# One GLA output sum's split moved into four small-pool buffers, and the first MLP block's last products placed behind LN1's transposes of token tiles three and four

## The chip, the core and the metric

The kernel runs on one core of a Trainium2 chip. The metric is the device time of one execution in microseconds. It is 865.92 us before the change, the median of three runs (865.25 to 866.03). Lower is better.

## What is computed

The reference is one decoder layer on 512 tokens of width 1024, in float32. Cut to what matters here:

```python
h = layer_norm(x, ln_in_g, ln_in_b)
q_g, k_g, v_g, r_g, a_lr, q_lat, kv_lat, gate_logits = split(h @ w_in)
y_gla = (rms_norm(gla(q_g, k_g, v_g, log_a)) * silu(r_g)) @ w_o_gla
q  = rms_norm(q_lat) @ w_q_b            # 8 heads, 128 without and 64 with rope
kv = rms_norm(kv_lat) @ w_kv_b          # 8 heads, keys 128 and values 128
y_mla = softmax_attention(q, kv) @ w_o_mla
mix = (g_gla * y_gla + g_mla * y_mla) @ w_out
h1 = layer_norm(ALPHA * h + mix, ln1_g, ln1_b)
out = layer_norm(ALPHA * h1 + square(relu(h1 @ w_ff1)) @ w_ff2, ln2_g, ln2_b)
```

## The kernel before

**Arithmetic.** Every float32 matrix product is made of three TensorE products. An operand is split into a high part `hi` (a rounding copy on ScalarE, ACT in the profile) and a low part `lo` (a subtraction on VectorE, DVE). The products are hi by hi, hi by lo and lo by hi. They are the three lines L280 to L282 (features by tokens, `gemm_fm`), L318 to L320 (tokens by features, `gemm_tm`) and L1320 to L1322 (the units below).

**Weights as a stream.** All weights stand in one list, `stream`, in the order of use. `fetch` (L196) allocates a raw tile `wraw` and issues its load on SyncE's queue (SP in the profile). `pump` (L211) fetches two entries ahead and splits one or two entries ahead of the entry in use. The raw tiles rotate through three buffers, the split parts `whi` and `wlo` through two each. An entry's `home` names the buffers that receive its split. Home "w" is `whi` and `wlo`. Home "r" is `wraw` twice, so the two parts of such an entry sit in two of the three raw buffers until its last product has read them. Pool A has large tiles (4 KB per partition), pool B has 22 small ones (2 KB per partition).

**Units.** Some matrix products (`unit`, L1297) use seven products of half-size blocks in place of eight, with operands that are sums of blocks. `yg`, the GLA output projection with `w_o_gla`, is one of them. Its products are named "11", "t1", "22", "t2", "t3", "21" and "t4", each with two column groups g = 0 and 1. A name with t stands for a sum of weight blocks. Such a sum is made in a tile `wq` and then split like loaded weights. With `cut` = 2 the split of a `yg` entry is made in two halves.

**Order around the first edit.** The stream has `yg` "22" and "t2", then the rope part of the queries (`qr`, group 0), then `yg` "t3" (groups 0 and 1), then for the first pair of MLA heads `qn` (two entries), `kn` and `mv` (one each, from `w_kv_b`), then `yg` "21", which is loaded as it is, then `qr` group 1. In the trace, `latT` are the normalised latents, which SP loads back from memory (L1435) into tiles of pool A. `ogT` are the operands of `yg`. `QS<-q` (L1071) are 16 copies of the roped queries, issued on GpSimd's queue (POOL). `mv`'s products are L318 to L320, those of `kn` and `qn` L280 to L282.

**Order around the second edit.** After the mixer, the rows `res` are normalised by LN1 two token tiles at a time. `ln1(1)` (L1540) does token tiles three and four. DVE and POOL make the statistics, DVE normalises the rows, and `ln_transpose` (L509) transposes them on TensorE (L516, PE in the profile), eight channel blocks of two transposes each. ACT makes the high part `h`, DVE the low part. Meanwhile TensorE multiplies the first block of `w_ff1` with the first 256 tokens (L1556, 8 contraction blocks of 12 products of 256 columns) and then with the last 256 tokens, whose operands those transposes deliver.

```python
    t_ln = spawn(ln1(1))
    accs = gemm_fm(PL["f1", 0, 0], h1T, T, None, toks=slice(0, 256))
    finish(t_ln)
```

A `spawn`ed generator is advanced at every `tick`, so its instructions stand between those of the products. A scheduler then sets the order on each engine by its own estimates, with data dependences and the edges that `tc.issue_after` adds.

Of the kernel before, what the change touches and what calls it, by code (L numbers as in the profile page):

```python
# [11 lines left out]
F32R = mybir.dt.float32r  # L12
# [7 lines left out]
P = 128  # L20
T = 512
# [31 lines left out]
def tile_hybrid_block(ctx: ExitStack, tc: tile.TileContext, I, out, dbg=None):  # L53
# [12 lines left out]
    def nm(s):  # L66
        uid[0] += 1
        return f"{s}_{uid[0]}"
# [4 lines left out]
    def A(shape, dt=F32, n="a"):  # L73
        tag, bufs = ("C", 8) if n in TAG_C else (n, TAG_W[n]) if n in TAG_W else ("A", 24)
        return pa.tile(shape, dt, tag=tag, bufs=bufs, name=nm(n))

    def B(shape, dt=F32, n="b"):
        return pb.tile(shape, dt, tag="B", name=nm(n))
# [8 lines left out]
    def MM(n="mm"):  # L87
        return pm.tile([P, T], F32, tag="mm", name=nm(n))
# [4 lines left out]
    def f(ap):  # L93
        return ap.bitcast(F32)
# [28 lines left out]
    mm = nc.tensor.matmul  # L123
# [46 lines left out]
    st = {"dma": 0, "spl": 0, "gates": ()}  # L170
# [25 lines left out]
    def fetch(n):  # L196
        while st["dma"] < min(len(stream), n):
            e = stream[st["dma"]]
            st["dma"] += 1
            if "src" in e:  # L200
                continue
            raw = A([P, e["nk"], T * 2 // e["nk"]], F32, e.get("at", "wraw"))
            for sl, src, cw in e["dmas"]:
                if cw is None:
                    dst = raw[:, sl, :e["n"]]
                else:
                    dst = raw[:, sl[0], sl[1]].rearrange("p (h c) -> p h c", c=cw)
                nc.sync.dma_start(dst, src)
            e["raw"] = raw

    def pump(i):  # L211
        fetch(i + 1 + DMA_AHEAD)
        while st["spl"] < min(len(stream), i + 2 + SPLIT_AHEAD):
            e = stream[st["spl"]]
            if st["spl"] > i + e.get("ahead", SPLIT_AHEAD) and not e["res"]:
                break
            nk, n = e["nk"], e["n"]
            hi, lo = [A([P, nk, T * 2 // nk], F32R, w) for w in HOME["a" if e["res"] else e.get("home", "w")]]
            raw = e["src"]() if "src" in e else e.pop("raw")
            with ExitStack() as gates:  # L220
                for g in e.get("gates") or st["gates"] or (st.get("pt", ()) if e.get("late") else ()):
                    gates.enter_context(tc.issue_after(g.ins))
                step = 1 if e.get("fine") else nk // e.get("cut", 1)
                for k in [slice(i, i + step) for i in range(0, nk, step)]:
                    st["ins"] = act(hi[:, k, :n], raw[:, k, :n], AF.Copy)
                    st["lo"] = vtt(lo[:, k, :n], raw[:, k, :n], f(hi[:, k, :n]), op=ALU.subtract)
            st["gates"] = ()
            e["w"] = (hi, lo)
            if "post" in e:
                e["post"](raw)  # L230
            if "post2" in e:
                later[st["spl"] + 2] = lambda p=e["post2"], r=raw: p(r)
            later.pop(st["spl"], lambda: None)()
            st["spl"] += 1
# [32 lines left out]
    def part(x, i, c):  # L267
        return x[i][:, c] if isinstance(x, tuple) else x[:, i, c]

    def gemm_fm(pl, xs, n, evac, width=None, toks=slice(0, T), accs=None, guard=None):  # L270
        na = n // P
        accs = accs or [MM() for _ in range(na)]
        for k in range(pl["nk"]):
            hi, lo = weights(pl, k)
            xh, xl = part(xs[k], 0, toks), part(xs[k], 1, toks)
            first, last = k == 0, k == pl["nk"] - 1
            for a in range(na):
                c = slice(a * P, (a + 1) * P)
                o = accs[a][:, toks]
                mm(o, hi[:, c], xh, start=first, stop=False)  # L280
                mm(o, hi[:, c], xl, start=False, stop=False)  # L281
                mm(o, lo[:, c], xh, start=False, stop=last)  # L282
            if not last:
                tick(width)
        if guard:
            guard()
        if evac is not None:
            for a in range(na):
                evac(a, accs[a])
                if a == na // 2 - 1:  # L290
                    pump(pl["idx"][-1] + 1)
        tick(width)
        return accs
# [45 lines left out]
    PL = {}  # L339
# [16 lines left out]
    for op, _ in RW:  # L356
        for hf in range(2):
            PL["r"].append(len(stream))
            e = {"nk": 2, "n": T, "res": False, "ahead": 2, "home": "wwwwrwrwrwwwrw"[2 * RW.index((op, _)) + hf]}
# [11 lines left out]
    HOME = {"w": ("whi", "wlo"), "r": ("wraw", "wraw"), "a": ("xh", "xl")}  # L371
# [29 lines left out]
    def plan_unit(*seq):  # L401
        for key, op in seq:
            for g in range(UNITS[key][2]):
                PL[key, op, g] = len(stream)
                e = {"nk": 4, "n": 256, "res": False}
                if key in ("g1","yg"):
                    e["cut"] = 2
                if (key, op, g) == ("yg", "t3", 1):
                    e["home"] = "r"
                if op[0] != "t" and (op, key) not in HELD:  # L410
                    e["dmas"] = [(slice(0, 4), u_src(key, int(op[0]) - 1, int(op[1]) - 1, g), None)]
                else:
                    e["src"] = lambda q=(key, (op, g)): WQ[q]
                    if key == "g0" and op in ("t1", "t2"):
                        e["ahead"], e["home"] = 2, "wr"[g]
                if op == ("t1" if key == "g0" else "22"):
                    e["post"] = lambda raw, q=(key, "t1", "t2", g): u_sum(*q, WQ[q[0], ("22", q[3])] if q[0] == "g0" else raw)
                    if key == "f1":
                        e["post2"] = lambda raw, q=(key, "12", "t3", g): u_sum(*q, raw)
                elif op == "21" and key == "yg":  # L420
                    e["post"] = lambda raw, g=g: u_sum("yg", "t2", "t4", g, raw)
                elif op == "t2" and key == "g1":
                    e["post"] = lambda raw, g=g: u_acc("g1", "t2", "t4", g, "21")
                elif op == "t2" and key != "yg":
                    e["post2" if key == "f1" else "post"] = lambda raw, q=(key, "t2", "t4", g): u_sum(*q, WQ[q[0], ("21", q[3])])
                stream.append(e)
# [82 lines left out]
    def ln_transpose(rows, g, b, outs, hf, alt=False, n="h0"):  # L509
        tk = slice(hf * 256, (hf + 1) * 256)  # L510
        for k in range(NK):
            if len(outs) <= k:
                outs.append(A([P, 2, T], F32R, n) if n == "h0" else (B([P, T], F32R, n), B([P, T], F32R, n)))
            p = MM() if alt and k in (4, 5) else PX()
            for i in range(2):
                tp = nc.tensor.transpose(p[:, i * P:(i + 1) * P], rows[2 * hf + i][:, k * P:(k + 1) * P],  # L516
                                         identJ if hf and n == "h0" else ident)
            if n == "h0" and k == 1:
                st["tp"] = tp
            tmp = B([P, 256], F32, "lnt")  # L520
            hi, lo = part(outs[k], 0, tk), part(outs[k], 1, tk)
            ha = act(hi, p[:, :256], AF.Identity, scale=g[:, k:k + 1], bias=b[:, k:k + 1])
            if (alt or n == "h1") and k % 2:
                act(tmp, p[:, :256], AF.Identity, scale=g[:, k:k + 1], bias=b[:, k:k + 1])
            else:
                vts(tmp, p[:, :256], g[:, k:k + 1], b[:, k:k + 1], op0=ALU.mult, op1=ALU.add)
            hd = vtt(lo, tmp, f(hi), op=ALU.subtract)
            if n == "h1":
                st["ln"] = (ha, hd)
            elif hf and k == 5:  # L530
                st["h0"] = (ha, hd)
            yield hd
# [691 lines left out]
    for hf in range(2):  # L1224
# [8 lines left out]
        for i in range(2):  # L1233
            gemm_tm([PL["lat", i]], hT, half, ev_lat(i), tts=(2 * hf, 2 * hf + 1), guard=lat_guard if i and not hf else None,
                    held=i and not hf)
# [245 lines left out]
    class Lazy:  # L1481
        def __getitem__(self, h):
            while omT[h] is None:
                tick(2)
            return omT[h]
# [18 lines left out]
    res = []  # L1504
# [33 lines left out]
    h1T = []  # L1538
# [14 lines left out]
    finish(t_ln)  # L1553
    st["gates"] = st["ln"]
    t_ln = spawn(ln1(1))
    accs = gemm_fm(PL["f1", 0, 0], h1T, T, None, toks=slice(0, 256))  # L1556
    finish(t_ln)

    def residual1():
# [147 lines left out]
    for ci in range(FC):  # L1707
# [3 lines left out]
        if ci == 0:  # L1711
            lo = stream[PL["f1", 0, 0]["idx"][2]]["w"][1]
# [32 lines left out]
        else:  # L1745
# [31 lines left out]
            tt, r, bst = 3, res[3], S([P, 4, 6], F32, "bst4")  # L1777
# [3 lines left out]
            for c0, n in ((0, T), (T, 256), (T + 256, 256)):  # L1781
                last = c0 > T
                acc = end if last else MM()[:, :n]
                ws = slice(c0 % T, c0 % T + n)
                for k in range(nb):
                    hi, lo = weights(PL["f2last"][c0 // T], k)
                    xh, xl = hid[k][:, 0, tt * P:], hid[k][:, 1, tt * P:]
# [58 lines left out]
```

## Time and profile before

| what | value |
|---|---|
| median of 3 runs | 865.92 us (865.25 to 866.03) |
| the profiled execution's own time | 866.7 us |
| its span, first to last instruction | 864.9 us |
| PE busy | 852.7 us, 99% |
| DVE busy | 657.8 us, 76% |
| ACT busy | 494.5 us, 57% |
| POOL busy | 136.0 us, 16% |
| HBM traffic over the span | 142 GB/s |
| granted TensorE clock, mean | 0.998 |

A row of the timeline gives the start in us from the beginning of the span, the duration in us, the engine, the line, the operation, what it writes and reads, its form and a count. In brackets stands the idle time of the engine just before it and what ended that. SPq and POOLq are the queues that issue DMAs. Matmuls overlap each other, so the pace of TensorE is read from the starts and not from the durations.

### The profile page before, as it was taken

The numbers are of one execution on the slowest core, as the hardware profiler recorded it, in microseconds if no ns is written. First come the engines' busy times: TensorE is split into PE (matmuls) and PEld (weight loads), VectorE is DVE, ScalarE is ACT, GpSimd is POOL, SyncE is SP. The second block draws the span as 40 slices with busy tenths as digits, with TensorE's granted clock in tenths as the row PEclk, the third lists the DMA queues.
The fourth block names the chain that finished last, engine by engine and source line by source line (L and its number), as shares of the span: only waits on it lengthen the run. The fifth ranks groups of instructions, "written<-read, shape, count | busy, mean of one in ns | idle before, by whom it ended". The sixth has DMA issues, their size and how long they took to land.

```text
span 864.9 us, 13264 instructions
## 1 busy us (share of the span) xinstructions
PE 852.7 (99%) x4887; PEld 752.6 (87%) x4887; DVE 657.8 (76%) x1169; ACT 494.5 (57%) x891; POOL 136.0 (16%) x179
## 2 busy tenths in 40 slices
PE   8999999999999999999999999999999999999996
PEld 7988888889999998988888889988888888889985
DVE  7767889977578967997856978985567546897865
ACT  7456977655576854565745334475466446766820
POOL 1530001110222103030000021005301520141000
PEclk9999999999999999999999999999999999999999
DMA  9995946696649817133146455009912990499312
GB/s 319 228 213 159 341 153 163 213 264 214 147 145 242 204 32 187 50 104 98 37 176 214 126 166 184 1 0 272 253 59 51 299 218 17 102 244 234 112 62 75
DMA packets 101231, 137.94 MB, mean 159 GB/s; under 512 B 13201, under 2 KB 66116, under 8 KB 101168
## 3 DMA queue, kind: packets, MB, share of 16 engines
q1 hardware_dynamic: 76512, 91.35, 33.9%
q0 software_dynamic: 22784, 41.10, 22.8%
q10 hardware_dynamic: 1872, 4.66, 1.4%
q8 instruction: 38, 0.62, 0.3%
q14 instruction: 25, 0.20, 0.1%
HBM read 113.49 MB, written 8.91 MB: 142 GB/s over the span
## 4 chain that ended last, share of the span: by engine, by line
PE 97%; DMA 1%; ACT 1%; DVE 1%; issue 0%; POOLq 0%; POOL 0%; DVEq 0%; SPq 0%; ACTq 0%
PE mm L280 10%; PE mm L281 10%; PE mm L282 10%; PE mm L1322 6%; PE mm L1320 6%; PE mm L1321 6%; PE mm L320 5%; PE mm L318 5%; PE mm L319 5%; PE px L1654 3%; PE px L1656 3%; PE px L1655 3%; PE mm L1654 2%; PE mm L1656 2%; PE mm L1655 2%; PE mm L876 1%
## 5 line engine op out<-in xcount | busy, mean ns | idle before, releaser
L111 DVE TENSOR_TENSOR wlo<-wraw,whi 128x1024 fp32r<-128x1024 f32 (+2 forms) x108 | 96.9, 912 | 66.5 <-ACT whi L111 66.4
L111 ACT ACTIVATE whi<-wraw 128x1024 fp32r<-128x1024 f32 (+2 forms) x108 | 85.0, 806 | 75.7 <-PE mm L281 19.6
L281 PE MATMUL mm<-h,whi 128*128 128x512 f32 x224 | 87.2, 389 | 0.0
L280 PE MATMUL mm<-h,whi 128*128 128x512 f32 x224 | 87.1, 390 | 0.0
L111 DVE TENSOR_TENSOR wlo<-wq,whi 128x1024 fp32r<-128x1024 f32 (+1 forms) x66 | 63.6, 980 | 28.1 <-ACT whi L111 28.1
L282 PE MATMUL mm<-h,wlo 128*128 128x512 f32 x224 | 83.2, 390 | 0.0
L111 ACT ACTIVATE whi<-wq 128x1024 fp32r<-128x1024 f32 (+1 forms) x66 | 55.3, 860 | 32.0 <-PE mm L1321 15.3
L1673 POOL DMA_DIRECT2D res<-ev x42 | 38.4, 1042 | 178.8 <-ACT ev L111 145.5
L1320 PE MATMUL mm<-sh,whi 128*128 128x256 f32 x176 | 49.9, 284 | 0.0
L1321 PE MATMUL mm<-sh,whi 128*128 128x256 f32 x176 | 49.7, 283 | 0.0
L282 PEld LDWEIGHTS mm<-h,wlo 128*128 128x128 f32 x224 | 42.0, 188 | 8.8
L281 PEld LDWEIGHTS mm<-h,whi 128*128 128x128 f32 x224 | 42.1, 188 | 8.7
L280 PEld LDWEIGHTS mm<-h,whi 128*128 128x128 f32 x224 | 42.0, 188 | 8.7
L1322 PE MATMUL mm<-sh,wlo 128*128 128x256 f32 x176 | 49.5, 283 | 0.0
L111 ACT ACTIVATE relu<-mm 128x512 f32<-128x512 f32 x26 | 15.2, 594 | 42.0 <-PE mm L282 42.0
L111 ACT ACTIVATE xh<-wraw 128x1024 fp32r<-128x1024 f32 (+1 forms) x24 | 24.2, 1014 | 25.5 <-PE mm L320 15.5
L111 DVE TENSOR_TENSOR xl<-wraw,xh 128x1024 fp32r<-128x1024 f32 (+1 forms) x24 | 27.9, 1170 | 10.9 <-ACT xh L111 10.9
L1321 PEld LDWEIGHTS mm<-sh,whi 128*128 128x128 f32 x176 | 33.8, 192 | 0.0
L1320 PEld LDWEIGHTS mm<-sh,whi 128*128 128x128 f32 x176 | 33.8, 192 | 0.0
L1322 PEld LDWEIGHTS mm<-sh,wlo 128*128 128x128 f32 x176 | 33.6, 192 | 0.0
L1322 PE MATMUL mm<-h,wlo 128*128 128x256 f32 x112 | 32.1, 287 | 0.0
L1320 PE MATMUL mm<-h,whi 128*128 128x256 f32 x112 | 31.8, 284 | 0.0
(493 smaller groups left out, 2783.9 us busy)
## 6 DMA issues: line engine op xcount, KB each, us to landing
wraw<-in_w_ff_dram SPq DMA_DIRECT2D x36, 512.0 KB, 5.0
wraw<-in_w_in_dram SPq DMA_DIRECT2D x30, 512.0 KB, 4.8
wq<-in_w_ff_dram POOLq DMA_DIRECT2D x26, 512.0 KB, 9.9
res<-ev POOLq DMA_DIRECT2D x42, 256.0 KB, 9.8
wq<-in_w_in_dram POOLq DMA_DIRECT2D x20, 512.0 KB, 9.8
wq<-in_w_in_dram SPq DMA_DIRECT2D x18, 512.0 KB, 7.8
hsd<-hs SPq DMA_DIRECT2D x16, 256.0 KB, 3.8
xr<-hsd SPq DMA_DIRECT2D x16, 256.0 KB, 3.7
```

The source lines that it names most:

```text
L111: ins = op(*a, **k)
L280: mm(o, hi[:, c], xh, start=first, stop=False)
L281: mm(o, hi[:, c], xl, start=False, stop=False)
L282: mm(o, lo[:, c], xh, start=False, stop=last)
L318: mm(o, xh, hi[:, :n], start=opens, stop=False, skip_group_check=share)
L319: mm(o, xh, lo[:, :n], start=False, stop=False, skip_group_check=share)
L320: mm(o, xl, hi[:, :n], start=False, stop=last, skip_group_check=share)
L1320: mm(oa, hi[:, k, c], xh, start=opens and k == 0 and a == 0, stop=False, skip_group_check=True)
L1321: mm(oa, hi[:, k, c], xl, start=False, stop=False, skip_group_check=True)
L1322: mm(oa, lo[:, k, c], xh, start=False, stop=k == 3, skip_group_check=True)
L1654: mm(o, xh[:, c], hi[:, pp], start=opens, stop=False, skip_group_check=True)
L1655: mm(o, xh[:, c], lo[:, pp], start=False, stop=False, skip_group_check=True)
```

## The change

Two edits, and a helper class.

1. The split of `yg` "t3", group 1, gets home "b": its high part goes to two tiles `bh` of pool B and its low part to two tiles `bl`, each of 2 by 256 columns. The raw buffers are no longer used for it. `Halves` indexes the pair like one tile.
2. In the first `w_ff1` product on the first 256 tokens, the first hi by hi product of the last contraction block gets an `issue_after` edge to the transpose of the second channel block (`st["tp"]`), for each of the four output blocks. `ln_transpose` now records this transpose for LN1 too.

```diff
+    class Halves(list):
+        def __getitem__(self, at):
+            p, k, c = at
+            if isinstance(k, slice):
+                return list.__getitem__(self, k.start // 2)[p, :, c]
+            return list.__getitem__(self, k // 2)[p, k % 2, c]
...
-            hi, lo = [A([P, nk, T * 2 // nk], F32R, w) for w in HOME["a" if e["res"] else e.get("home", "w")]]
+            if e.get("home") == "b":
+                hi, lo = [Halves([B([P, 2, 256], F32R, w) for _ in range(2)]) for w in ("bh", "bl")]
+            else:
+                hi, lo = [A([P, nk, T * 2 // nk], F32R, w) for w in HOME["a" if e["res"] else e.get("home", "w")]]
...
-    def gemm_fm(pl, xs, n, evac, width=None, toks=slice(0, T), accs=None, guard=None):
+    def gemm_fm(pl, xs, n, evac, width=None, toks=slice(0, T), accs=None, guard=None, held=False):
...
-                mm(o, hi[:, c], xh, start=first, stop=False)
+                with ExitStack() as gates:
+                    if last and held:
+                        gates.enter_context(tc.issue_after(st["tp"].ins))
+                    mm(o, hi[:, c], xh, start=first, stop=False)
...
                 if (key, op, g) == ("yg", "t3", 1):
-                    e["home"] = "r"
+                    e["home"] = "b"
...
-            if n == "h0" and k == 1:
+            if k == 1:
                 st["tp"] = tp
...
-    accs = gemm_fm(PL["f1", 0, 0], h1T, T, None, toks=slice(0, 256))
+    accs = gemm_fm(PL["f1", 0, 0], h1T, T, None, toks=slice(0, 256), held=True)
```

No instruction is added on PE. The class stands above `pump`, so in the changed kernel L280 to L282 are L293 to L295, L318 to L320 are L331 to L333, L516 is L529 and L1435 is L1448.

**The loads on SP.** Before, the two loads of `latT` stand ahead of the second `qn` entry (`wraw_3905`), `kn` (`wraw_3943`) and `mv` (`wraw_3956`). The two rows from `in_w_o_gla_dram` are `yg` "21".

```order
L208 DMA wraw_3830<-in_w_q_b_dram 128x2x128
L1435 DMA latT_3703<-latd_1180 128x1024
L1435 DMA latT_3705<-latd_1220 128x1024
L208 DMA wraw_3905<-in_w_q_b_dram 128x2x128 x2
L208 DMA wraw_3943<-in_w_kv_b_dram 128x2x128 x2
L208 DMA wraw_3956<-in_w_kv_b_dram 128x2x128 x2
L208 DMA wraw_3978<-in_w_o_gla_dram 128x4x256
```

After the change the same place on SP reads:

```order
L208 DMA wraw_3830<-in_w_q_b_dram 128x2x128
L208 DMA wraw_3907<-in_w_q_b_dram 128x2x128 x2
L208 DMA wraw_3945<-in_w_kv_b_dram 128x2x128 x2
L1448 DMA latT_3703<-latd_1180 128x1024
L1448 DMA latT_3705<-latd_1220 128x1024
L208 DMA wraw_3958<-in_w_kv_b_dram 128x2x128 x2
L208 DMA wraw_3980<-in_w_o_gla_dram 128x4x256
```

The second `qn` entry and `kn` have moved ahead of the two `latT` loads; `mv` still stands behind them.

**TensorE at `kn` and `mv`.** Before, the first two products of `mv` (L318) stand among the twelve of `kn` (`px_3987` and `px_3988`).

```order
L280 MATMUL px_3988<-latT_3703,whi_3959 128x512
L281 MATMUL px_3988<-latT_3703,whi_3959 128x512
L318 MATMUL mm_4016<-whi_3980,latT_3703 128x256
L318 MATMUL mm_4023<-whi_3980,latT_3703 128x256
L282 MATMUL px_3987<-latT_3703,wlo_3960 128x512
L282 MATMUL px_3988<-latT_3703,wlo_3960 128x512
L280 MATMUL px_3987<-latT_3705,whi_3959 128x512
```

After the change the end of `kn` and the start of `mv` read:

```order
L293 MATMUL px_3990<-latT_3705,whi_3961 128x512
L294 MATMUL px_3990<-latT_3705,whi_3961 128x512
L295 MATMUL px_3990<-latT_3705,wlo_3962 128x512
L331 MATMUL mm_4018<-whi_3982,latT_3703 128x256
L331 MATMUL mm_4025<-whi_3982,latT_3703 128x256
L332 MATMUL mm_4018<-wlo_3983,latT_3703 128x256
L333 MATMUL mm_4018<-whi_3982,latT_3703 128x256
```

All twelve products of `kn` now stand ahead of `mv`'s first one.

**TensorE at the second edit.** Before, the last contraction block of the first 256 tokens (`xh_6044`) ends ahead of the eight transposes, and the first product of the last 256 tokens (`xh_5746`) follows them at once.

```order
L282 MATMUL mm_5987<-h_1157_5905,xl_6045 128x256
L516 MATMUL px_6028<-ca,res_5518 128x128
L516 MATMUL px_6035<-ca,res_5518 128x128
L516 MATMUL px_6060<-ca,res_5518 128x128
L516 MATMUL px_6067<-ca,res_5518 128x128
L516 MATMUL px_6028<-ca,res_5532 128x128
L516 MATMUL px_6035<-ca,res_5532 128x128
L516 MATMUL px_6060<-ca,res_5532 128x128
L516 MATMUL px_6067<-ca,res_5532 128x128
L280 MATMUL mm_5984<-h_1129_5824,xh_5746 128x256
```

After the change the last transposes and what follows them read (`h_1159_5907` is the last contraction block's operand):

```order
L529 MATMUL px_6062<-ca,res_5534 128x128
L529 MATMUL px_6069<-ca,res_5534 128x128
L293 MATMUL mm_5986<-h_1159_5907,xh_6046 128x256
L294 MATMUL mm_5986<-h_1160_5908,xh_6046 128x256
L295 MATMUL mm_5986<-h_1159_5907,xl_6047 128x256
L293 MATMUL mm_5987<-h_1159_5907,xh_6046 128x256
```

The twelve products of the last contraction block now stand between the eight transposes and the first product of the last 256 tokens.

## The prediction

> **What bounds the kernel now.** I read the page first: how much of the span TensorE is idle at all.
>
> ```profile
> span 864.9 us, 13264 instructions
> PE 852.7 (99%) x4887; PEld 752.6 (87%) x4887; DVE 657.8 (76%) x1169; ACT 494.5 (57%) x891; POOL 136.0 (16%) x179
> ```
>
> TensorE (PE) is busy for 852.7 of 864.9 us. No product is removed, so only time in which PE stands can be won, 12.2 us at most. The view of the waits says who makes PE stand (engine, line, waited for: total us, times, longest).
>
> ```profile
> PE mm L318 <- ACT whi L111: 1.5, 1, 1.5
> ...
> PE mm L280 <- ACT PT L111: 0.6, 1, 0.6
> ```
>
> The first is at edit 1; the wait at edit 2 is shorter and shown below. In the timeline of PE, the first stands between the first four of the twelve products of `kn` (`px`) and the first of `mv`:
>
> ```profile
> 334.59 0.40 PE L280 MATMUL px<-latT,whi 128*128 128x512 f32 x1
> 334.82 0.39 PE L281 MATMUL px<-latT,whi 128*128 128x512 f32 x1
> 336.67 0.51 PE L318 MATMUL mm<-whi,latT 128*128 128x256 f32 x2 [1.46 <-ACT whi L111]
> 337.01 0.63 PE L282 MATMUL px<-latT,wlo 128*128 128x512 f32 x2
> ```
>
> Ordinary starts of 512-column products are 0.23 us apart (334.59 to 334.82), so `kn` began at 334.13, three steps before. From 334.82 to 336.67 it is 1.85, so 1.62 us are lost. The chain of waits says by what:
>
> ```profile
> 331.52 4.36 DMA wraw<-in_w_kv_b_dram
> 335.98 0.64 ACT whi L111
> ```
>
> The load of `mv`'s weights lands late and its split runs only then. Why it starts at 331.5 is in SP's timeline and in SP's own waits between 300 and 350 us:
>
> ```profile
> 322.32 2.77 SPq L1435 DMA_DIRECT2D latT<-latd  x2
> 325.20 0.90 SPq L208 DMA_DIRECT2D wraw<-in_w_q_b_dram  x2
> 330.08 1.91 SPq L208 DMA_DIRECT2D wraw<-in_w_kv_b_dram  x4
> 332.15 2.83 SPq L208 DMA_DIRECT2D wraw<-in_w_o_gla_dram  x2
> ```
> ```profile
> SPq L1435 <- DVE wraw L111: 11.2, 1, 11.2
> SPq L208 <- PE mm L1322: 4.0, 1, 4.0
> ```
> ```profile
> L1322 PE MATMUL mm<-ogT,wraw x8: 283/283/364, 324.4 to 329.9; 128*128 128x256 f32 x8
> ```
>
> SP waits 4.0 us for a product L1322 and issues `kn`'s and `mv`'s loads at 330.08: these are two of the three raw buffers, held by the "t3" split until its last product, which starts at 329.9. That is what edit 1 releases.
>
> **Edit 1, first the split itself.** ACT and DVE execute as many pieces as before (two each), at another place. Their rows:
>
> ```profile
> 320.63 0.62 ACT L111 ACTIVATE tabw<-sn 128x512 f32<-128x512 f32 x1
> ...
> 326.77 0.63 ACT L111 ACTIVATE q<-rt 128x512 fp32r<-128x512 f32 x1 [1.48 <-DVE rt L111]
> ...
> 329.42 0.63 ACT L111 ACTIVATE whi<-wraw 128x512 fp32r<-128x512 f32 x1 [2.01 <-PE mm L1321]
> ```
> ```profile
> 319.76 0.69 DVE L111 TENSOR_TENSOR wlo<-wraw,whi 128x512 fp32r<-128x512 f32 x1 [1.12 <-ACT whi L111]
> ...
> 320.97 1.28 DVE L111 TENSOR_TENSOR wraw<-wq,wraw 128x512 fp32r<-128x512 f32 x2
> ...
> 335.17 0.68 DVE L111 SCALAR_TENSOR_TENSOR qn<-mm,qn 128x512 fp32r<-128x512 f32 x1
> ```
>
> The order puts `bh` behind the second `tabw`, so from about 321.2 to 322.4 (two pieces of 0.63), and `bl` on DVE from about 321.9 to 323.2 (1.28 us for the two). Apart from two early ones, the products of this sum are taken from 324.4 (first start in the row of L1322), so the split is covered by 1.2 us. If that cover were gone, the cost would be what `bl` is late, 1.28 us at most. What waits behind `bl` is SP: the first `latT` load needs the `wq` tile that `bl` reads. It goes out at about 323.3 in place of 322.32, and `kn` wants it at 334.13.
>
> The two early products are the price on PE. They fill a wait there:
>
> ```profile
> 320.35 0.30 PE L1320 MATMUL mm<-ogT,wraw 128*128 128x256 f32 x1
> 320.49 0.28 PE L1321 MATMUL mm<-ogT,wraw 128*128 128x256 f32 x1
> 320.61 0.40 PE L282 MATMUL mm<-latT,wlo 128*128 128x512 f32 x1
> ```
>
> The L282 behind them needs a low part that DVE finishes at 320.45 (319.76 + 0.69). In the new order PE waits for it instead and starts L282 at about 320.53, 0.08 earlier, and runs the two later for 0.12 each. Cost: 0.24 - 0.08 = **0.16 us** (between 0 and 0.24).
>
> **Edit 1, then the loads.** The second `qn` entry now takes the buffer of the first `qr` entry, `kn` that of the second (split ended at 320.45), `mv` that of the first `qn` entry, which DVE splits at about 325.2. On SP `mv` stands behind both `latT` loads, the second of which went out by 325.09 (322.32 + 2.77). So `mv` is issued at about 325.5, 6 us earlier than at 331.52. With its 4.36 us it lands by about 330. Next late is its split, for two reasons. The high part needs the `whi` buffer of the second `qn` entry, whose products end where `kn`'s begin: 334.13 + 0.16, so the high part is there at about 335.1 (0.63). The low part stands on DVE behind `qn`, which ended at 335.85 (335.17 + 0.68); two sums now stand behind `kn`'s low part and not ahead of it, but the pause for `kn`'s weights goes, so I put `mv`'s low part at 335.85 + 0.69 = 336.5, give or take 0.3. PE comes to `mv` after `kn`'s twelve products, 334.29 + 12 x 0.23 = 337.1, and wants the low part 0.24 later. Both are in time, the low part by 0.5 to 1.1 us. So the 1.62 us go, and with them about 0.10 us by which the first pair after the pause runs slower (336.67 to 337.01 holds two products of 0.12 each). Gain: **1.72 us** (1.2, if the low part is 0.5 late, to 1.72).
>
> **Is the lead kept?** `yg` "21" is next. Its second group is where PE could catch up with a load:
>
> ```profile
> 346.39 0.28 PE L1322 MATMUL mm<-ogT,wlo 128*128 128x256 f32 x1
> ```
> ```profile
> 345.20 0.69 DVE L111 TENSOR_TENSOR wlo<-wraw,whi 128x512 fp32r<-128x512 f32 x1 [2.58 <-ACT whi L111]
> ```
> ```profile
> 331.00:345.00 14.00, 12.54 (x80) 11.13 (x79) 9.20 (x16) 5.58 (x11) 7.38 (x15) 1.00 0.88 205
> ```
> ```profile
> wraw<-in_w_o_gla_dram SPq DMA_DIRECT2D x2, 512.0 KB, 8.2
> ```
>
> The split of that group starts only when its load has landed, and its low part is ready at 345.89, 0.5 us ahead of PE's need at 346.39. A lead of 1.56 us is kept whole if the landing moves forward by 1.06 us or more. In that stretch the DMA engines are 0.88 busy at 205 GB/s. `kn` and `mv`, 2 x 256 KB, leave it for the quiet time before 331: 0.52 MB / 205 GB/s = 2.6 us less in front of "21". The buffers for "21" come free earlier too: the first group's with the split of 329.42 (0.63, then 0.69 on DVE), at about 331 in place of the issue at 332.15. I take 1.5 to 2.5 us, enough.
>
> The Trainium skill, in "DMA: Bandwidth & Descriptors", section "Queues, rings and completion order", says that each DMA engine takes turns between queues packet by packet. By that, what SP's loads gain is partly taken from the `QS` copies, and the loads of "21" would still meet them. The trace shows the contention (512 KB in 8.2 us here), but not who gives way; it speaks for the first rival below. By the rule the time would be nearer to that rival's 864.5 than to 863.6.
>
> Later waits, such as the 0.6 us for `PT`, hang on PE's own results and move with it. Edit 1 in all: -1.72 + 0.16 = **-1.56 us**.
>
> **Edit 2.** PE at the transposes, and DVE's normalisation of the rows:
>
> ```profile
> 536.45 1.03 PE L516 MATMUL px<-ca,res 128*128 128x128 f32 x8
> 537.82 0.74 PE L280 MATMUL mm<-h,xh 128*128 128x256 f32 x4 [0.33 <-ACT h L111]
> 538.40 0.44 PE L516 MATMUL px<-ca,res 128*128 128x128 f32 x2
> 538.86 0.39 PE L281 MATMUL mm<-h,xh 128*128 128x256 f32 x1
> ```
> ```profile
> 532.79 1.53 DVE L111 TENSOR_SCALAR res<-res,mv 128x1024 f32<-128x1024 f32 x2
> ```
>
> The starts of the eight transposes are (1.03 - 0.27) / 7 = 0.11 apart, so without waiting the next product starts at 537.32; it starts at 537.82: 0.50 lost. Behind the next two transposes another 0.18 is lost, waiting for the first low part, and the first pair after each pause runs about 0.10 slower: 0.88 us together. After the change twelve products of 0.12 = 1.44 us stand between. The first operand takes 0.93 us from its second transpose (536.45 + 4 x 0.11 = 536.89) to 537.82, and then stands ready 0.9 us before PE wants it; the first low part, 1.04 us later still on the old clock, is wanted 0.7 us after that. Gain: **0.88 us** (0.5 to 0.9).
>
> The added edge makes PE take the transposes 1.44 us earlier, at 535.01. Everything on PE is queued behind them. They need DVE's rows, ready at 534.32 (532.79 + 1.53). Margin 0.69 us; each us of lateness beyond that costs one, where before the products covered it.
>
> **Sum.** -1.56 - 0.88 = -2.44 us; I take 0.1 back for a pause that leaves a trace. The profiled execution would take 866.7 - 2.3 = 864.4, and the median, 0.8 below it, 865.92 - 2.3 = **863.6 us**.
>
> **Rivals.**
>
> 1. *The load of "21" becomes the wait.* If its second group lands as late as before, PE gains only the 0.5 us of slack there: 865.92 - 0.5 - 0.88 = 864.5. For it: DMA is 0.88 busy and the `QS` copies compete. Against: 0.5 MB leaves the stretch and the issue moves forward. Landing 1.06 us earlier decides. Chance 0.17.
> 2. *The transposes wait for the rows.* Edit 2 gives nothing or little: 865.92 - 1.5 = 864.4. For it: the margin is only 0.69 us, on a DVE that stands busy there. Against: DVE's rows follow PE's products, so they move with PE. Chance 0.10.
> 3. *Slower: the small pool runs short.* Four of 22 buffers are held from 321.2 to the sum's last product at 330.2. If a later small tile, `q` (ACT at 326.77 above) say, takes its turn in one of these, ACT and DVE stop until 330.2, 3.4 us, and so do the splits queued behind it; PE then loses that less the 0.88 of edit 2: 868.4. It decides from a delay of 2.4 us on. Against: the order of `rt` and `q` is unchanged. Chance 0.05.
> 4. *More: the lead also closes the 0.6 us wait for `PT`.* 863.0. For it: DVE, which feeds that place, starts earlier once "21" lands earlier. Chance 0.10.
>
> My forecast has 0.58.
>
> **The numbers.** About 0.2%, 1.7 us, is what a measurement of this kernel can tell from no change, so faster means below 864.2. Forecast and rival 4 lie there, with 0.06 off for the uncertain terms: 0.62. Rivals 1 and 2 and that 0.06 are within it, 0.33. Slower 0.05. The range goes from rival 4 with the spread of the runs below it (0.3), 862.7, to edit 2 alone with edit 1's lead wholly lost, 865.92 - 0.88 = 865.0, and the spread: 865.3.
>
> **What would show it.** Right: no wait of L331 (`mv`) for `whi`; `mv`'s load issued near 325.5; no wait of L293 for `h` after the transposes; the starts of late stages about 2.3 us earlier. Wrong: a new wait at `yg` "21" (rival 1), one before L529 (rival 2), an ACT or DVE pause near 327 (rival 3), or a lead of 1.5 us at 345 that is gone at 480.

## The result and the profile after

The kernel took 865.92 us in the runs shown ahead of the prediction; timed side by side, 17 runs each, it took **866.03 us before (865.25 to 867.29) and 864.16 us after (864.03 to 864.93)**: a ratio of 0.998, 95% interval 0.9972 to 0.9987. That is 1.87 us, just over the 0.2% that can be told from no change. Forecast were 863.6 us in a range of 862.7 to 865.3. The profiled execution of after took 864.0 us at a span of 862.2. Its page begins:

```profile
span 862.2 us, 13265 instructions
PE 852.3 (99%) x4887; PEld 752.8 (87%) x4887; DVE 658.1 (76%) x1169; ACT 494.0 (57%) x891; POOL 136.0 (16%) x179
```

No work went; 2.7 us of span did. The waits of PE (engine, line, waited for: total us, times, longest) no longer name `mv`'s first product, nor `h` behind the transposes; the wait for `PT` is as it was:

```profile
PE wake L167 <- DVE still L164: 1.5, 1, 1.5
PE mm L293 <- ACT PT L111: 0.6, 1, 0.6
PE px L529 <- DVE x L111: 0.4, 1, 0.4
PE px L529 <- ACT x L111: 0.3, 1, 0.3
```

SP's timeline shows the loads at edit 1: `kn`'s two (first row), the `latT` loads, `mv`'s two, and the two of "21".

```profile
320.30 0.88 SPq L208 DMA_DIRECT2D wraw<-in_w_kv_b_dram  x2
322.94 2.14 SPq L1448 DMA_DIRECT2D latT<-latd  x2
325.18 0.90 SPq L208 DMA_DIRECT2D wraw<-in_w_kv_b_dram  x2
330.85 2.37 SPq L208 DMA_DIRECT2D wraw<-in_w_o_gla_dram  x2
```

`mv`'s load starts at 325.18 where 325.5 was forecast (331.05 before). PE's timeline, from the last products of `kn` to `mv`, has no gap left: each 512-column product starts 0.23 us behind the one ahead of it.

```profile
336.43 0.39 PE L294 MATMUL px<-latT,whi 128*128 128x512 f32 x1
336.66 0.39 PE L295 MATMUL px<-latT,wlo 128*128 128x512 f32 x1
336.89 0.40 PE L331 MATMUL mm<-whi,latT 128*128 128x256 f32 x2
337.12 0.28 PE L332 MATMUL mm<-wlo,latT 128*128 128x256 f32 x1
```

DVE's timeline has the split of `bl` and `mv`'s low part, ready at 335.88 + 0.68 = 336.56, 0.56 us ahead of L332 at 337.12:

```profile
321.62 1.29 DVE L111 TENSOR_TENSOR bl<-wq,bh 128x512 fp32r<-128x512 f32 x2
...
335.88 0.68 DVE L111 TENSOR_TENSOR wlo<-wraw,whi 128x512 fp32r<-128x512 f32 x1
```

The stretch from 331 to 345 us (after its length: busy time and count of PE, PEld, DVE, ACT, POOL; granted clock, DMA share, GB/s), and the second load of "21", issued at 332.85 (334.61 before). Here is the window's row, and then what the line L208 shows for that one load:

```profile
331.00:345.00 14.00, 14.00 (x91) 12.86 (x90) 11.72 (x20) 6.90 (x13) 7.31 (x15) 1.00 0.77 184
```
```profile
L208 SPq DMA_DIRECT2D wraw<-in_w_o_gla_dram x1: 368/368/368, 332.9 to 332.9; - x1
...
DMA to landing us min/median/max: 6.4/6.4/6.4
```

The DMA engines are 0.77 busy where they were 0.88, and the load lands after 6.4 us where it took 9.8. At edit 2, PE's timeline has the eight transposes, then the twelve held products, then the last 256 tokens (535.58) with no gap:

```profile
533.15 0.28 PE L295 MATMUL mm<-h,xl 128*128 128x256 f32 x1
533.27 1.04 PE L529 MATMUL px<-ca,res 128*128 128x128 f32 x8
534.06 0.36 PE L293 MATMUL mm<-h,xh 128*128 128x256 f32 x1
...
535.46 0.28 PE L295 MATMUL mm<-h,xl 128*128 128x256 f32 x1
535.58 0.65 PE L293 MATMUL mm<-h,xh 128*128 128x256 f32 x4
```

To compare many executions, I sum PE's lost time over a stretch from these timelines: by how much its starts lie further apart than the ordinary step (0.23 us for 512 columns, 0.12 for 256). In the two profiles it fell from 2.05 to 0.52 us between 300 and 340 (edit 1: 1.53) and from 1.04 to 0.11 between 500 and 540 (edit 2: 0.93); 0.17 went in the first 20 us, where nothing was changed. That is 2.63 of the 2.7 us. But the median fell by 1.87 only. This gap is what the experiments had to settle.

### The profile page after: what moved, and what is told of

It is laid out like the page before. It is cut to its first block, busy times and chain, and to the rows that moved or that the text cites. A ratio compares the mean times of both kernels' runs of the same rounds, so it can differ in the third digit from the quotient of the medians.

```text
span 862.2 us, 13265 instructions
## 1 busy us (share of the span) xinstructions
PE 852.3 (99%) x4887; PEld 752.8 (87%) x4887; DVE 658.1 (76%) x1169; ACT 494.0 (57%) x891; POOL 136.0 (16%) x179
## 4 chain that ended last, share of the span: by engine, by line
PE 97%; ACT 1%; DVE 1%; DMA 0%; issue 0%; POOLq 0%; POOL 0%; DVEq 0%
PE mm L293 10%; PE mm L295 10%; PE mm L294 10%; PE mm L1335 6%; PE mm L1333 6%; PE mm L1334 6%; PE mm L333 5%; PE mm L331 5%; PE mm L332 5%; PE px L1668 3%; PE px L1667 3%; PE px L1669 3%; PE mm L1668 2%; PE mm L1667 2%; PE mm L1669 2%; PE mm L887 1%
## 5 line engine op out<-in xcount | busy, mean ns | idle before, releaser
L293 PE MATMUL mm<-h,whi 128*128 128x512 f32 x224 | 87.1, 390 | 0.0
L295 PE MATMUL mm<-h,wlo 128*128 128x512 f32 x224 | 83.2, 390 | 0.0
L293 PEld LDWEIGHTS mm<-h,whi 128*128 128x128 f32 x224 | 42.1, 188 | 8.7
L295 PEld LDWEIGHTS mm<-h,wlo 128*128 128x128 f32 x224 | 42.0, 188 | 8.7
```

## The experiments

They were run in three groups, each on one chip beside before itself. Medians in us:

| group | before | kernels |
|---|---|---|
| 1 | 865.61 | e1 865.16, e2 864.73, e3 865.02, e4 869.02 |
| 2 | 865.98 | e5 864.19, e6 865.81, e7 864.41, e8 864.81 |
| 3 | 865.53 | e9 865.63, e10 865.15, e11 864.73, e12 864.29 |

A ratio against before has an interval of about 0.0009 to either side, 0.8 us. With the first measurement, before itself came out between 865.53 and 866.03, after between 864.16 and 864.29. The whole change was thus worth 1.87, 1.79 (e5) and 1.24 us (e12).

The texts recorded ahead of the runs speak of theories. In A the terms of the prediction add up in every execution, in B the wait for `mv`'s load was longer in the profiled execution of before than in most, in C edit 1's lead is used up by a later wait.

### The two edits apart (e1, e2, and again e10, e11 beside e12)

e1 and e10 are after without the hold; e2 and e11 are after with the split back in the raw buffers:

```
-    accs = gemm_fm(PL["f1", 0, 0], h1T, T, None, toks=slice(0, 256), held=True)
+    accs = gemm_fm(PL["f1", 0, 0], h1T, T, None, toks=slice(0, 256))
```
```
-                    e["home"] = "b"
+                    e["home"] = "r"
```

> Edit 1 alone (the first MLP block's last products are not held). Theory A, the terms of the prediction add up in every execution: edit 1 is worth 1.5 us, so about 864.5; in the profile no wait of L331 (mv) for whi, and the two waits of edit 2's place (0.8 and 0.3 us before L529 and L293 near 537) still there. Theory B, the wait for mv's load was longer in the profiled execution of before (1.46 us) than in most: the medians fell by 1.87 us and the two profiles' spans by 2.7, so edit 1 is worth only about 0.9 in the median, 865.1, and what it does besides is to narrow the spread of the runs: before 865.25 to 867.29, this about 1 us. Theory C, edit 1's lead is used up before 534 by another wait: the time of before, 866.0.

> Edit 2 alone (the split of t3's second group stays in the raw buffers). All theories give edit 2 0.9 us, so about 865.1, and no wait of L293 for h after the transposes. Theory A: the wait of mv's first product (L331) for whi is 1.4 to 1.5 us as in before's profile. Theory B: that wait differs from run to run (0 to 2 us), this profile may show another one than 1.46, its kv_b loads and o_gla loads between 331 and 345 land at other times, and the runs spread over about 2 us as before's do.

> Edit 1 alone again, now on the same chip as edit 2 alone and both. Edit 2's worth is the difference to both: 0.9 to 1.0 us by all theories, since the pauses behind the transposes are the same in every profile.

> Edit 2 alone again, on the same chip as both. Edit 1's worth in the median is the difference to both. Theory A: 1.5 us. Theory B, worked out from the run without the QS copies (1.57 us under before, of which 0.76 are the wait for PT that went with them, so that mv's wait was worth 0.8 in before's median, less the 0.2 that edit 1 costs near 320): 0.5 to 0.7 us. The wait of L331 in this profile is a further sample, 0 to 1.5.

> The changed kernel, on the same chip as its two halves: 1.4 to 1.9 us under before; the two halves' worths add up to that within 0.3.

Measured against before: e1 -0.45, e2 -0.88; in group 3 e10 -0.38 (0.9994, 0.9985 to 1.0003), e11 -0.80 (0.9992, 0.9983 to 1.0001), e12 -1.24 (0.9987, 0.9978 to 0.9995). In group 3 edit 2 is worth 865.15 - 864.29 = 0.86 and edit 1 864.73 - 864.29 = 0.44; they add up within 0.1. Of the expectations, e12's (1.4 to 1.9 us under before) was missed with 1.24, edit 2's 0.9 to 1.0 and theory B's 0.5 to 0.7 for edit 1 narrowly. Edit 1 gives 0.4 to 0.5 us in these medians; the intervals of e1 and e10 reach to 1.2 and 1.3 us, just short of theory A's 1.5; theory B's 0.9 for e1 was about twice what came. Why theory A fails stands in the waits of PE of e2 and of e11, whose code at `mv` is that of before:

```profile
PE mm L331 <- ACT whi L111: 0.3, 1, 0.3
```
```profile
PE mm L331 <- ACT whi L111: 0.2, 1, 0.2
```

Same order, same buffers, and a wait of 0.3 and 0.2 us in place of 1.5. What differs is how long `mv`'s load takes. The rows of L208 for `mv`'s two halves, from issue to landing; first before, then e2, then e11:

```profile
DMA to landing us min/median/max: 2.6/3.5/4.4
```
```profile
DMA to landing us min/median/max: 2.7/2.9/3.2
```
```profile
DMA to landing us min/median/max: 2.6/2.8/3.1
```

The second half (the largest number) took 4.4 us in the profiled execution of before and 3.2 and 3.1 here. The spread of e1's runs (1.38 us) is hardly below e2's (1.46), so what theory B said of the spreads was not borne out by these eleven runs each. Before and after with equally many runs spread over 2.0 and 0.9 us (17 each), and over 1.9 (e6) and 1.3 (e5, 11 each).

### Each kernel once more (e5, e6)

> The changed kernel itself once more, beside the next three on one chip. Theory B (mv's load lands at another time in each execution while its buffers come free late; edit 1 is worth the 0.3 us of pause left in a good execution and 1.5 in a bad one) expects: 0.9 to 1.9 us under before, no wait at L331 again, mv's load landing 6 us or more ahead of PE's need, and a spread of the runs of about 1 us, what is left of it from the waits for the first rows of x. Theory A (the terms add in every execution) expects 2.3 to 2.6 us under before.

> The kernel before itself once more, as a second sample of its wait and as a measure of what no change gives: a ratio of 1.000. Theory B: the wait of mv's first product (L318) for whi is again another than 1.46 us, anywhere from 0 to 2, with the issue of mv's second load within 0.3 us of 331.5 and its landing 3 to 5 us later; the span less the waits for x and for mv is the same as in the first profile within 0.3. Theory A: 1.3 to 1.5 us again.

e5: 864.19, a ratio of 0.9979 (0.997 to 0.9988), 1.79 us under before; no wait at L331. e6, which is before: 865.81, ratio 0.9997 (0.9988 to 1.0006). In e6's profile `mv`'s second half lands 2.9 us after its issue, and its first product starts 0.45 us behind the one ahead, with an ordinary step of 0.23:

```profile
334.89 0.39 PE L281 MATMUL px<-latT,whi 128*128 128x512 f32 x1
335.34 0.51 PE L318 MATMUL mm<-whi,latT 128*128 128x256 f32 x2
```

So 0.2 us of wait, a third sample beside e2 and e11. Yet its execution took 866.8, no less than the first, since another load was late: a `w_ff` load ended a wait of ACT near 518, and PE waited 0.9 us at the transposes of the first two tiles for what ACT had queued behind that split (ACT's row, then PE's wait):

```profile
518.46 1.06 ACT L111 ACTIVATE whi<-wraw 128x1024 fp32r<-128x1024 f32 x1 [1.53 <-DMA wraw<-in_w_ff_dram]
```
```profile
PE px L516 <- ACT lnt L111: 0.9, 1, 0.9
```

The expected sameness of the rest of the span did therefore not hold: its lost time between 500 and 540 is 2.46 us and not 1.04. The two long executions had different causes.

### Before without the copies that share the DMA (e7)

```
             for h in range(4):
+                if g == 0:
+                    QS[h] = parts[h // 2][h % 2]
+                    continue
                 q = B([P, T], F32R, "QS")
```

> The kernel before, with the 16 copies of 64 KB that build QS for the first four heads left out (those heads take the unrotated tiles as they stand, so their scores are other numbers). If mv's load lands late and at other times because it shares the DMA engines with these copies: its second half lands 2.5 to 3.2 us after its issue, the wait at L318 is 0.3 us or less, and the time is 0.5 to 1.5 us under before with a narrower spread. Rival: it is the load of the next sum (512 KB, issued 0.6 us behind mv on the same queue) that it shares them with, or the memory: landing 3.2 to 4.4 us after the issue, the wait 0.3 to 1.5 as before.

864.41 us, 1.57 under before (0.9984, 0.9975 to 0.9992), and PE takes `mv` without a pause. L208's row for `mv`'s halves:

```profile
DMA to landing us min/median/max: 2.4/2.5/2.5
```

At the edge of the range expected (the time is just past its 1.5), and the shortest of all: in this one execution the load of "21" was still behind `mv` on the queue, and without the copies it did not hurt. The Trainium skill, in "DMA: Bandwidth & Descriptors", section "Queues, rings and completion order", has the DMA engines take turns between queues packet by packet; the row fits that, 2.5 us with SP's queue alone and 2.9 to 4.4 with the copies on the other one, though no row shows the turns themselves. Of the pause before the product that waits for `PT`, 0.76 us went here too; why was not found out. The rest of 1.57, 0.81, is an estimate of what `mv`'s wait was worth in that group's median; it takes a pause of one profile from a difference of medians.

### The raw buffers freed in other ways (e3, e4)

e3 puts the split into the usual pair, e4 the first group into the raw buffers and the second into the pair:

```
                 if (key, op, g) == ("yg", "t3", 1):
-                    e["home"] = "b"
+                    e["home"] = "w"
```
```
-                if (key, op, g) == ("yg", "t3", 1):
-                    e["home"] = "b"
+                if (key, op, g) == ("yg", "t3", 0):
+                    e["home"] = "r"
```

> Both edits, but the split of t3's second group goes to the usual pair of split buffers (whi, wlo) and not to the small pool: the raw buffers come free as early, and four small buffers less are used. If the early release of the raw buffers is the cause of edit 1's gain: no wait at mv (L331), mv's load issued before 328.5, and 864.2 within 0.3. Rival: the place of the split matters, since the pair's two buffers are wanted by qn's splits, whose second entry must then wait for t3's last product near 329.9 and has its low part near 331.2 with PE there at 331.6; with 0.5 us of delay PE waits 0.1 to 0.5 us before qn's second entry: 864.3 to 864.7.

> Both edits, but the first group of t3 is split in place in the raw buffers and the second in the pair: the first group's products are taken early (in the order they stand among the first products of q), so the raw buffers come free some 4 to 6 us earlier than in before without any other home. If the release time of the raw buffers is what counts: mv's load issued by 327, no wait at L331, 864.2; and as products fill the pause of 0.44 us near 320, down to 863.8. Rival: the early split has no cover (its sum must be loaded and added earlier) and PE waits for it near 319 to 321: 864.5 to 865.5.

e3: 865.02 us, 0.3 above e2 of its group, above both ranges expected. `mv`'s load goes out at 328.61 and its wait is gone, as the first theory said, but the time is not that of after. No run of after stands in this group, and 0.3 us is little beside the interval of 0.8, so the profile has to say it: lost between 300 and 340 are 1.30 us in place of 0.52, part of it at `qn`'s second entry, as the rival had it (0.23), and most at a place that neither named, the first product of "21", for which ACT's split comes late:

```profile
337.33 0.40 PE L331 MATMUL mm<-whi,latT 128*128 128x256 f32 x2
338.02 0.39 PE L1333 MATMUL mm<-ogT,whi 128*128 128x256 f32 x1 [0.29 <-ACT whi L111]
```

e4: 869.02 us (five runs; 1.0034, 1.0022 to 1.0047), slower by far more than either theory had. Its products did fill the pause near 320, but the rotation of `q` came late on DVE, and `qn`'s first product waited for it. DVE's timeline and then PE's:

```profile
326.07 1.29 DVE L111 TENSOR_TENSOR wlo<-wq,whi 128x512 fp32r<-128x512 f32 x2 [4.11 <-ACT whi L111]
...
331.85 1.28 DVE L111 TENSOR_TENSOR rt<-mm,tab 128x512 f32<-128x512 f32 x2
```
```profile
332.68 0.47 PE L293 MATMUL mm<-latT,whi 128*128 128x512 f32 x1 [2.62 <-DVE rt L111]
```

Freeing the buffers early is not enough; the place that a split takes in the rows of ACT and DVE decides as well.

### Rivals 2 and 3 made true (e8, e9)

e8 holds the last two contraction blocks, e9 takes eight small buffers:

```
-                    if last and held:
+                    if held and k >= pl["nk"] - 2:
```
```
-                if (key, op, g) == ("yg", "t3", 1):
+                if (key, op) == ("yg", "t3"):
                     e["home"] = "b"
```

> Both edits, but the products of the last two contraction blocks are held behind the transposes, 24 and not 12. The pauses behind the transposes are gone already, so nothing can be won; the transposes go 1.44 us earlier, to 531.8, and DVE's rows are ready at 532.6: PE waits 0.7 to 0.8 us before L529, and the time is 0.7 above the changed kernel's (rival 2 of the prediction, made true). Against it: if the rows are ready earlier than DVE's records say, or DVE has slack there, no difference.

> Both edits, and the first group of t3 is split into the small pool too: eight of its 22 buffers are held from about 321 to 330 and not four. This is rival 3 of the prediction with twice its strength. If the small pool is near its end: ACT or DVE stops near 327 (at the q or rt tiles) until t3's last product near 330, and the time is 1 to 4 us above the changed kernel's. If the pool has slack: no such pause, the pair of split buffers comes free for qn's entries earlier, and the time is the changed kernel's within 0.4.

e8: 864.81 us, 0.62 above e5 beside it. PE's timeline, and DVE's row for the rows of the two tiles:

```profile
531.81 0.28 PE L295 MATMUL mm<-h,xl 128*128 128x256 f32 x1
532.10 1.29 PE L529 MATMUL px<-ca,res 128*128 128x128 f32 x8
533.15 0.37 PE L293 MATMUL mm<-h,xh 128*128 128x256 f32 x1
```
```profile
531.15 1.53 DVE L111 TENSOR_SCALAR res<-res,mv 128x1024 f32<-128x1024 f32 x2
```

Rival 2 is real, one block further on: the first transposes start 0.29 us behind the product ahead of them and not 0.12, as soon as the first tile's rows are there, and the others are stretched to the second tile's (532.68). The margin of the change as made is used by 24 held products, and was enough for 12.

e9: 865.63 us, 1.3 above e12, of which 1.0 is lost between 300 and 340. But no engine stopped from 327 until 330: the small pool has room for eight. What cost time, as I read the rows, is ACT's order, where the splits of `kn` and `mv` (`x2` below) now stand together behind two `e` pieces; `kn`'s was at 331.47 in after, ahead of them:

```profile
332.94 1.08 ACT L111 ACTIVATE e<-mm 128x512 f32<-128x512 f32 x2
333.90 1.16 ACT L111 ACTIVATE whi<-wraw 128x512 fp32r<-128x512 f32 x2
```

So the 1 to 4 us expected of a pool that runs short were met in size, by another mechanism: rival 3's was not seen even with twice its buffers.

e9 shows one thing more. Its load of `mv` goes out at 324.33, about as early as in after, but PE takes `mv`'s first two products in the order of before, after four products of `kn`:

```profile
335.39 0.40 PE L294 MATMUL px<-latT,whi 128*128 128x512 f32 x1
335.63 0.40 PE L331 MATMUL mm<-whi,latT 128*128 128x256 f32 x2
```

They start 0.24 us behind the product ahead of them: in this profile the early load alone, without the new order on PE, leaves no wait for `mv`'s high part.

## Why the prediction was right in its time, and wrong in one step

The fall forecast was 2.3 us; 1.87, 1.79 and 1.24 were measured. The way and the two places were right. That the time lies in the range says less: the range went up to edit 2 alone, so it would have held with edit 1 worth nothing in the end.

- **Edit 1, the course of events: right.** The raw buffers were released, `mv`'s load went out at 325.18 (325.5 forecast), its low part was ready at 336.56 (336.5), PE came at 336.89 (337.1), and no wait was left; `bl` ended at 322.91 (323.2). Lost between 300 and 340 in all six profiles with this edit as made: 0.51 to 0.53 us. What released PE, the earlier load or the new order, is taken up below.
- **Edit 1, the two products moved: right.** Forecast 0.16, between 0 and 0.24. In e7, where nothing waits for `mv` and the products stand as before, 0.31 us are lost there; with the edit 0.52. Cost 0.21.
- **Edit 1, the size: wrong.** The step "-1.72 + 0.16 = -1.56 us" is right for the profiled execution (1.53), and "the median, 0.8 below it" took it over into the median whole. The page's execution was 0.8 us above the median, and I took that for a constant. It was in good part this very wait: 1.46 us there, 0.2 to 0.3 in the three other profiles of that code. So the term that failed is edit 1's gain of 1.72 us, taken at its full size for the median. In medians edit 1 gave 0.44 (group 3), about 0.6 by e7 (0.81 - 0.21), and 0.9 to 1.0 if edit 2's 0.88 of group 1 is taken from the 1.79 of e5 and the 1.87 of the first measurement. The three other profiles alone would give less than any of these: between 300 and 340 they lose only 0.1 to 0.3 us more than after does. How often the wait is long in the timed executions is not shown. With the 0.8 taken off the term (1.56 - 0.8 = 0.76) and edit 2's 0.88, the forecast would have been 864.3; 864.16 was measured.
- **Is the lead kept: right.** Forecast was a landing 1.5 to 2.5 us earlier. In the first two profiles it came at 332.85 + 6.4 = 339.3 where it was 344.4, 5.2 earlier: 1.8 by the earlier issue and 3.4 by the duration. But these 5.2 us are a sample too. In the three other profiles with before's code at `mv` (e6, e11, e2) the load took 7.4, 8.7 and 8.9 us and landed at 341.7 to 343.3; in the six with this edit as made it took 6.4 to 6.9 and landed at 339.3 to 340.4. Rival 1 didn't come. What the rule of the Trainium skill spoke for, that SP's gain would in part be taken from the `QS` copies, did show, but only in the first of them. The loads of "21" go out 1.3 to 1.8 us earlier and meet the three copies issued near 331 to 332. The rows of these three, of before and then of after:

```profile
DMA to landing us min/median/max: 3.2/3.2/3.2
```
```profile
DMA to landing us min/median/max: 5.3/5.4/5.5
```

All sixteen copies of this stretch, of before and then of after:

```profile
DMA to landing us min/median/max: 1.9/6.0/8.3
```
```profile
DMA to landing us min/median/max: 2.1/4.6/6.6
```

The first three lost some 2 us each, the sixteen together gained, and none of it reached PE.

- **Edit 2: right.** 0.93 us in the profiles (0.88 forecast), 0.86 in the medians of group 3. The margin of 0.69 us to the rows was there, by DVE's row in after and the transposes at 533.27:

```profile
531.05 1.53 DVE L111 TENSOR_SCALAR res<-res,mv 128x1024 f32<-128x1024 f32 x2
```

The rows are ready at 532.58. e8 shows what lies behind the margin. Rival 2 didn't come.

- **Rival 3 didn't come,** and e9 shows no shortage even with eight buffers. **Rival 4 didn't come:** L293 waits 0.61 us for `PT` as before.

In part open: whether edit 1 removes the wait by the earlier load or by PE's order. The order of after wants `mv` at 336.89, that of before at 335.05. By e9 the earlier load is enough. The order alone might nearly be: the high part in e2, ready at 334.63 + 0.63 = 335.26 by ACT's row below, would have been in time for it, and in the first profile of before, the slowest, it was ready at 336.6, with the low part 0.2 us late for 337.12 (336.64 + 0.69 = 337.33 by DVE's row). A kernel with the new order and the late load was not made.

```profile
334.63 0.63 ACT L111 ACTIVATE whi<-wraw 128x512 fp32r<-128x512 f32 x1 [0.57 <-DMA wraw<-in_w_kv_b_dram]
```
```profile
336.64 0.69 DVE L111 TENSOR_TENSOR wlo<-wraw,whi 128x512 fp32r<-128x512 f32 x1 [0.79 <-ACT whi L111]
```

## What to carry to other kernels

A wait on a DMA in one profile is a sample: before its length goes into a forecast, ask how far that execution lies from the median, and count the excess only once. The wait of edit 2, whose 0.3 us for `h` stands in all five profiles without the hold, came out at its full size, and a hold has a margin that one more block can use up. Buffers freed early paid here only where the splits that use them kept their places on ACT and DVE.

## What the runs showed of the hardware that I had not expected

The same load, issued within 0.3 us of the same time by the same code, took 2.9, 3.1, 3.2 and 4.4 us to land in four executions, and 2.5 without the sixteen copies on POOL's queue. The 512 KB load behind it took 7.4 to 9.8 us in these four. With 0.5 MB moved out of the stretch, in which the DMA engines were 0.88 to 0.94 busy and then 0.72 to 0.84, it took 6.4 to 6.9 in six. The copies issued near 331 to 332 beside its first half landed after 5.0 to 5.6 us in these six and 3.0 to 4.2 in the four. I put that down to this half going out up to 1.3 us earlier; no run tests it.
